# Second product of the feed-forwards: three of four groups by jobs of seven products, and more adding transfers

## The chip, the cores and the metric

The kernel runs on one core of a Trainium2 chip. The core has TensorE (PE, matrix products), VectorE (DVE), ScalarE (ACT), GpSimd (POOL), SyncE (SP, which here only issues transfers) and 16 DMA engines. The metric is the device time of one execution in microseconds, given as the median of several runs.

## The reference

Two decoder layers work on 512 prompt tokens and 32 sample tokens together (T = 544 columns). Layer 0 mixes with a short convolution, layer 1 with retention over four heads. Each layer then adds a feed-forward, which is what the change is about:

```python
def swiglu(x, w_gate, w_up, w_down):
    return (jax.nn.silu(x @ w_gate) * (x @ w_up)) @ w_down
...
        x = x + m
        x = x + swiglu(rmsnorm(x, norm_ffn[i]), ffn_w_gate[i], ffn_w_up[i], ffn_w_down[i])
```

The model width is 1024 (8 tiles of 128), the inner width of the feed-forward 2816 (22 tiles of 128). "First product" below is the pair with w_gate and w_up, "second product" the one with w_down.

## The kernel before, in words

Everything lies transposed: x is eight tiles of 128 features by 544 tokens (line 122). Each fp32 operand of a product is split into a high part, rounded to the fp32r type, and the low remainder. A product then has three terms, high by high, high by low, and low by high, each a matmul of 128 x 128 weights with 272 columns, half of the tokens.

A split can be made in two ways. `split` (195) copies the high part on ScalarE and subtracts it on VectorE. `split_adding` (200) writes the negated high part into the low one on ScalarE and adds the source to it by a transfer from DRAM that accumulates, issued on GpSimd. `mixed` (429) does the first half of a weight's columns in the first way and the second half in the second way.

The first product of a feed-forward (`gate_up`, 603, and class `Job`, 473) does not multiply 2 x 2 blocks by eight products but by seven, in the manner of Strassen and Winograd: the blocks are the two halves of the output tiles and of the input width on the weights' side, and the two halves of the input width and of the tokens on the other. `weights7` (437) loads two matrices of 1024 columns, forms the sums of their blocks on VectorE, and splits everything. `Job.product` (488) issues 4 x 3 = 12 matmuls. A job starts with product 1 (`begin`, 503), goes on with 6, 5, 2 and 7 (`middle`, 508), and closes with 4 and 3 (`end`, 524). `run` (530) chains the jobs: the weights of the next are prepared, the middle of this one is issued, product 1 of the next, and then the end of this one. The results pass from PSUM through `take`: "u1" to "u3" are snapshots of a running sum, "c11" to "c22" finished blocks.

Every inner tile m (0 to 10) stands for the pair of tiles m and m + 11. Two jobs, gate and up, make the hidden activations of one m, and `tail` (586) splits them into `xh` and `xl`, which are free in the feed-forward (`hidden`, 578). The second product is done in groups of three m's: `down` (654), called from `after` (695) once the first job pair of the next group is through, takes for each of the 8 output tiles a weight of 768 columns (`group_weights`, 644), multiplies all six hidden tiles by it in both token halves (`project`, 173), and adds the result to x (`residual`, 280). The last group has two m's (9 and 10) and also prepares what follows the feed-forward.

The pools around this: `wts` has three buffers each for a loaded weight (tag w), its high part (wh) and its low part (wl); one job uses two of each. The pool `sw` has a single buffer for the sums (w2, w4) and their parts. The engines run their instructions in order, but that order is not the order of the text: the framework's planner places instructions by their dependences and its own costs, and `tc.issue_after` forces an order where one is wanted. All plain weight loads go through SP's queue, all adding transfers through GpSimd's.

## Time and profile before

| | us |
|---|---|
| runs of the kernel, median of 3 | 1460.26 |
| lowest, highest | 1457.29, 1460.7 |
| the profiled execution's own time | 1456.52 |
| its span, first to last instruction | 1454.8 |

A profile line of instructions names the source line, the engine, the operation, the tile that is written and the tiles that are read, the shape, and the count; then busy time, the mean of one in ns, and after a second bar the time for which the engine stood idle ahead of them, with what ended most of it. PE is TensorE's matmuls, PEld its weight loads, which overlap them. Matmuls are pipelined: one is listed with some 290 ns, though the next starts 125 ns after it. In the chain of waits a row is start, duration and what ran. In the timeline a row is start, duration, engine, line, operation; a bracket at its end is the idle time ahead of it and its cause. In a table by stretches the columns are named in its first line; a count stands behind each busy time. In a list of transfers stands the size of one and, where known, the median time from issue to landing. In the list of queues stand packets, megabytes, and the share of the 16 DMA engines' span.

### The profile page before, as it was taken

The numbers are of one execution on the slowest core, as the hardware profiler recorded it, in microseconds if no ns is written. First come the engines' busy times: TensorE is split into PE (matmuls) and PEld (weight loads), VectorE is DVE, ScalarE is ACT, GpSimd is POOL, SyncE is SP. The second block draws the span as 40 slices with busy tenths as digits, with TensorE's granted clock in tenths as the row PEclk, the third lists the DMA queues.
The fourth block names the chain that finished last, engine by engine and source line by source line (L and its number), as shares of the span: only waits on it lengthen the run. The fifth ranks groups of instructions, "written<-read, shape, count | busy, mean of one in ns | idle before, by whom it ended". The sixth has DMA issues, their size and how long they took to land.

```text
span 1454.8 us, 26342 instructions
## 1 busy us (share of the span) xinstructions
PE 1440.8 (99%) x10826; PEld 1366.3 (94%) x10826; DVE 985.2 (68%) x1556; ACT 674.5 (46%) x994; POOL 151.5 (10%) x191
## 2 busy tenths in 40 slices
PE   9999999999999999999999999999999999999997
PEld 9999999999999999999877888878899999999997
DVE  5655679847748648677566585666789848759554
ACT  5222466626526436766422313123476626536434
POOL 0100011101101003210000000000111101001002
PEclk9999999999999999999999999999999999999998
DMA  6222246635536434786544373545666635536422
GB/s 226 75 90 90 87 115 145 148 114 125 144 105 143 123 81 126 200 211 192 192 160 159 129 258 122 196 169 186 176 133 156 153 99 134 135 103 153 123 73 77
DMA packets 86041, 204.61 MB, mean 141 GB/s; under 512 B 8832, under 2 KB 26128, under 8 KB 85664
## 3 DMA queue, kind: packets, MB, share of 16 engines
q1 hardware_dynamic: 67744, 165.37, 34.8%
q0 software_dynamic: 15872, 30.75, 12.7%
q10 hardware_dynamic: 2304, 6.79, 1.3%
q8 instruction: 85, 1.39, 0.4%
q14 instruction: 36, 0.29, 0.1%
HBM read 176.14 MB, written 26.75 MB: 139 GB/s over the span
## 4 chain that ended last, share of the span: by engine, by line
PE 93%; issue 2%; DVE 2%; DMA 1%; POOL 1%; ACT 1%; DVEq 0%; POOLq 0%; ACTq 0%
PE sm L494 35%; PE mm L181 34%; PE sm L181 8%; PE sm L1047 2%; PE sm L1048 2%; PE sm L1049 2%; PE sm L169 2%; PE sm L170 1%; PE sm L171 1%; PE sm L1273 1%; PE mm L494 1%; PE mm L1055 1%; PE mm L1291 1%; DMA wl<-in_rtout_dram 0%; PE mm L1222 0%
## 5 line engine op out<-in xcount | busy, mean ns | idle before, releaser
L196 ACT ACTIVATE wh<-w 128x1024 fp32r<-128x1024 f32 (+4 forms) x120 | 109.3, 916 | 293.8 <-PE mm L181 206.0
L494 PE MATMUL sm<-oh,wh 128*128 128x272 f32 x768 | 222.5, 290 | 0.1
L494 PE MATMUL sm<-ol,wh 128*128 128x272 f32 x768 | 221.3, 288 | 0.0
L494 PE MATMUL sm<-oh,wl 128*128 128x272 f32 x768 | 220.8, 287 | 0.0
L282 DVE TENSOR_TENSOR x<-x,mm 128x544 f32<-128x544 f32 x91 | 65.4, 719 | 147.2 <-PE mm L181 147.2
L494 PE MATMUL sm<-oh,h 128*128 128x272 f32 x560 | 161.3, 288 | 0.0
L494 PE MATMUL sm<-oh,l 128*128 128x272 f32 x560 | 160.9, 288 | 0.0
L494 PE MATMUL sm<-ol,h 128*128 128x272 f32 x560 | 160.9, 287 | 0.0
L181 PE MATMUL mm<-xh,wh 128*128 128x272 f32 x756 | 157.5, 290 | 0.0
L181 PE MATMUL mm<-xl,wh 128*128 128x272 f32 x756 | 156.7, 288 | 0.0
L181 PE MATMUL mm<-xh,wl 128*128 128x272 f32 x756 | 156.4, 288 | 0.0
L432 ACT ACTIVATE wh<-w 128x1024 fp32r<-128x1024 f32 x103 | 109.2, 1060 | 89.6 <-PE sm L494 61.7
L494 PEld LDWEIGHTS sm<-oh,wh 128*128 128x128 f32 x768 | 144.2, 188 | 2.4 <-ACT gate L554 1.1
L494 PEld LDWEIGHTS sm<-oh,wl 128*128 128x128 f32 x768 | 144.9, 189 | 0.0
L494 PEld LDWEIGHTS sm<-ol,wh 128*128 128x128 f32 x768 | 144.3, 188 | 0.2 <-DVE ol L197 0.2
L197 DVE TENSOR_TENSOR wl<-w,wh 128x1024 fp32r<-128x1024 f32 (+4 forms) x120 | 127.0, 1063 | 23.2 <-ACT wh L196 21.7
L435 POOL DMA_DIRECT2D wl<-in_ffgu_dram x87 | 75.8, 871 | 635.5 <-ACT wl L434 249.9
L181 PEld LDWEIGHTS mm<-xh,wh 128*128 128x128 f32 x756 | 119.3, 189 | 3.7 <-DVE sl L197 0.9
L181 PEld LDWEIGHTS mm<-xh,wl 128*128 128x128 f32 x756 | 118.7, 189 | 0.3
L181 PEld LDWEIGHTS mm<-xl,wh 128*128 128x128 f32 x756 | 118.9, 189 | 0.0
L197 DVE TENSOR_TENSOR l<-w,h 128x1024 fp32r<-128x1024 f32 x104 | 98.8, 954 | 26.9 <-ACT h L196 25.0
L494 PEld LDWEIGHTS sm<-oh,h 128*128 128x128 f32 x560 | 105.4, 188 | 0.2 <-ACT oh L196 0.2
(319 smaller groups left out, 3318.2 us busy)
## 6 DMA issues: line engine op xcount, KB each, us to landing
w<-in_ffgu_dram SPq DMA_DIRECT2D x88, 512.0 KB
wl<-in_ffgu_dram POOLq DMA_DIRECT2D x87, 256.0 KB, 4.8
w<-in_ffdn_dram SPq DMA_DIRECT2D x96, 192.0 KB
S<-in_rets_dram SPq DMA_DIRECT2D x16, 1024.0 KB
out_rets_dram<-S SPq DMA_DIRECT2D x16, 1024.0 KB
w<-in_cvin_dram SPq DMA_DIRECT2D x21, 512.0 KB
w<-in_rtqk_dram SPq DMA_DIRECT2D x16, 512.0 KB
w<-in_rtg_dram SPq DMA_DIRECT2D x16, 512.0 KB
```

The lines of the kernel that those rows point to most:

```text
L169: nc.tensor.matmul(out, lh, rh, start=start, stop=False, skip_group_check=True)
L170: nc.tensor.matmul(out, lh, rl, start=False, stop=False, skip_group_check=True)
L181: last_product[0] = nc.tensor.matmul(half(pt, hf)[:, :HT], w[:, c], act[k][:, hf * HT : (hf + 1) * HT], start=(first and k == ks[0] and i ...
L196: h = nc.scalar.activation(dh, src, AF.Copy)
L197: last_low[0] = nc.vector.tensor_sub(dl, src, dh.bitcast(F32))
L282: last_residual[0] = nc.vector.tensor_add(xk, xk, p)
L432: nc.scalar.activation(wh, w, AF.Copy)
L435: nc.gpsimd.dma_start(wl[:, n:], src[:, n:], accum_op=ALU.add)
L494: last = nc.tensor.matmul(out, w[:, c], b, start=(first and k == 0 and i == 0), stop=(k == KP - 1 and i == 2), skip_group_check=True,)
L1047: nc.tensor.matmul(out, xh[kt][:, ts_], wh[:, cw], start=(kt == 0), stop=False)
L1048: nc.tensor.matmul(out, xh[kt][:, ts_], wl[:, cw], start=False, stop=False)
L1049: last = nc.tensor.matmul(out, xl[kt][:, ts_], wh[:, cw], start=False, stop=(kt == KT - 1))
```

## The change

The diff does five things.

1. Three of the four groups of the second product are made by jobs of seven products. `group_jobs` builds four jobs a group. A job covers two output tiles of x, the two halves of the inner width, and the two halves of the tokens, so its blocks are 384 columns of weights and its products 3 x 3 = 9 matmuls. The jobs are put into the chain of `run` behind the gate and up jobs of the next group's first m. The finished blocks are added to x in place; the snapshots go into `sqlast` and a new tile `snap`.
2. `tail` forms, for these groups, the four sums of the hidden blocks that the seven products need, and splits all seven operands into the tiles `parts` (the former `xh` and `xl` in one tile) and, for the third m of a group, two tiles of the pool `fp`. The low part of the four sums is made by an adding transfer from SBUF. The tail of m = 3, 6 and 9 is deferred until the group's jobs are through, since they still read the tiles that it writes.
3. `adds`: the gate and up jobs of all m but the first, and all group jobs, make both halves of their first weight's low part with `split_adding` in place of `mixed`.
4. In layer 1's first job, the copies of `weights7`'s sums are placed behind the last negation of the work ahead.
5. In the second mixer, the load of the next head's rotated keys is issued ahead of the load of the gate.

`down` is left for the last group alone and loses its special cases; the spare buffer of the gates computed ahead moves into the tile `snap`. The diff, shortened:

```diff
...
-    xh = [resid.tile([P, T], F32R, tag=f"xh{k}", name=f"xh{k}") for k in range(KT)]
-    xl = [resid.tile([P, T], F32R, tag=f"xl{k}", name=f"xl{k}") for k in range(KT)]
+    parts = resid.tile([P, 2 * KT, T], F32R, tag="parts", name="parts")
+    xh, xl = [[parts[:, i * KT + k, :] for k in range(KT)] for i in range(2)]
+    blocks_of_parts = parts.rearrange("p a (b c) -> p (a b) c", b=2)
...
-    last_low = [None]
+    last_low, last_minus = [None], [None]
...
     def split_adding(dh, dl, w, src):
...
-        nc.scalar.activation(dl, dh.bitcast(F32), AF.Copy, scale=-1.0)
-        nc.gpsimd.dma_start(dl, src, accum_op=ALU.add)
+        last_minus[0] = nc.scalar.activation(dl, dh.bitcast(F32), AF.Copy, scale=-1.0)
+        nc.gpsimd.dma_start(like(dl, src), src, accum_op=ALU.add)
+    def like(t, src):
+        return t.rearrange("p (s c) -> p s c", s=2) if len(src.shape) == 3 else t
...
     def mixed(wh, wl, w, src):
-        n = KP * P
+        n = w.shape[1] // 2
...
-        nc.gpsimd.dma_start(wl[:, n:], src[:, n:], accum_op=ALU.add)
-    def weights7(src1, src2, sw, adding=False, spare=None):
-        n = KP * P
+        nc.gpsimd.dma_start(wl[:, n:], src[:, 1, :] if len(src.shape) == 3 else src[:, n:], accum_op=ALU.add)
+    def weights7(src1, src2, sw, n, adding=False, spare=None, adds=False):
...
-        w4 = (spare or sw).tile([P, n], F32, tag="w4", name=nm("w4"))
+        pool, tag = spare or (sw, "w4")
+        w4 = pool.tile([P, n], F32, tag=tag, name=nm("w4"))
...
-            second_load[0], last_load[0] = last_load[0], nc.sync.dma_start(two[i], (src1, src2)[i])
+            src = (src1, src2)[i]
+            second_load[0], last_load[0] = last_load[0], nc.sync.dma_start(like(two[i], src), src)
...
-        p1 = parts2(2 * n)
-        (split_adding if adding else mixed)(*p1, w1, src1)
-        p2 = parts2(2 * n, sw, ("h2", "l2"))
-        split(*p2, w2)
+        behind, p1, p2 = last_minus[0], parts2(2 * n), parts2(2 * n, sw, ("h2", "l2"))
+        (split_adding if adding or adds else mixed)(*p1, w1, src1)
+        with tc.issue_after(behind.ins) if adding else ExitStack():
+            split(*p2, w2)
...
-        split(*p4, w4)
+        with tc.issue_after(behind.ins) if adding else ExitStack():
+            split(*p4, w4)
...
-        def __init__(self, srcs, operand, sw, take, third=None, spare=None):
+        def __init__(self, srcs, operand, sw, take, third=None, spare=None, ks=range(KP), adds=False):
...
-            self.third, self.spare = third or bank, spare
+            self.third, self.spare, self.ks, self.adds = third or bank, spare, list(ks), adds
...
         def prepare(self, adding=False):
-            self.w = weights7(*self.srcs, self.sw, adding, self.spare)
+            self.w = weights7(*self.srcs, self.sw, len(self.ks) * P, adding, self.spare, self.adds)
         def product(self, out, which, first):
...
-            for k in range(KP):
-                c = slice(k * P, (k + 1) * P)
+            for j, k in enumerate(self.ks):
+                c = slice(j * P, (j + 1) * P)
...
-                        start=(first and k == 0 and i == 0), stop=(k == KP - 1 and i == 2),
+                        start=(first and j == 0 and i == 0), stop=(j == len(self.ks) - 1 and i == 2),
...
+            up_ = c1.enter_context(tc.tile_pool(name=f"ffs{layer}", bufs=1, reuse_waits="tile"))
...
+            turned = {}
+            def seven(m):
+                if m % GROUP < 2:
+                    at = blocks_of_parts[:, 14 * (m % GROUP) : 14 * (m % GROUP) + 14, :]
+                    return [(t[:, 0:1, :], t[:, 1:3, :], t[:, 3:7, :]) for t in (at[:, :7, :], at[:, 7:, :])]
+                rest = [fp.tile([P, 5, HT], F32R, tag="f", name=nm("f")) for _ in range(2)]
+                return [
+                    (t[:, 4:5, :], blocks_of_parts[:, 28 + 2 * i : 30 + 2 * i, :], t[:, 0:4, :]) for i, t in enumerate(rest)
+                ]
             def tail(m, g, u):
-                hs, ls = hidden(m)
-                for i in range(2):
-                    split(hs[i], ls[i], u[:, i, :])
+                if m >= last[0]:
+                    hs, ls = hidden(m)
+                    for i in range(2):
+                        split(hs[i], ls[i], u[:, i, :])
+                    return
+                b, t = [v.rearrange("p a (b c) -> p (a b) c", b=2) for v in (u, g)]
+                (h1, h2, ht), (l1, l2, lt) = seven(m)
+                nc.vector.tensor_sub(t[:, 0:2, :], b[:, 1::2, :], b[:, 0:2, :])
+                split(h1, l1, b[:, 0:1, :])
+                split(h2, l2, b[:, 2:4, :])
+                nc.vector.tensor_sub(t[:, 2, :], b[:, 3, :], t[:, 0, :])
+                nc.vector.tensor_sub(t[:, 3, :], b[:, 2, :], t[:, 2, :])
+                nc.scalar.activation(ht, t, AF.Copy)
+                nc.scalar.activation(lt, ht.bitcast(F32), AF.Copy, scale=-1.0)
+                nc.gpsimd.dma_start(lt, t, accum_op=ALU.add)
+                turned[m] = [
+                    {1: p[0][:, 0, :], 2: p[1][:, 0, :], 3: p[1][:, 1, :],
+                     5: p[2][:, 0, :], 7: p[2][:, 1, :], 6: p[2][:, 2, :], 4: p[2][:, 3, :]}
+                    for p in ((h1, h2, ht), (l1, l2, lt))
+                ]
+            later = {}
+            def group_jobs(ms):
+                c = slice(ms[0] * P, (ms[-1] + 1) * P)
+                src = a["ffdn"][layer].rearrange("(s n) p c -> n p s c", s=2)
+                def job(n):
+                    made = {}
+                    def take(what, p):
+                        if what == "u3":
+                            made[3] = up_.tile([P, HT], F32, tag="snap", name=nm("snap"), bufs=1)
+                            nc.scalar.activation(made[3], p, AF.Copy)
+                            return
+                        if what[0] == "u":
+                            nc.scalar.activation(halves(sqlast)[:, int(what[1]) - 1, :], p, AF.Copy)
+                            return
+                        kt, hf = n + int(what[1]) - 1, int(what[2]) - 1
+                        at = x[kt][:, hf * HT : (hf + 1) * HT]
+                        nc.vector.tensor_add(at, at, p)
+                        if what == "c22":
+                            nc.vector.tensor_add(at, at, made[3])
+                            nc.vector.tensor_add(x[n], x[n], sqlast)
+                    return Job(
+                        [src[n + i][:, :, c] for i in range(2)], lambda k, which: [t[which] for t in turned[k]], sw, take,
+                        lambda: psum()[:, 0, :], ks=ms, adds=True,
+                    )
+                return [job(n) for n in range(0, KT, 2)]
...
-                        tail(m, g, u)
+                        if m and m % GROUP == 0:
+                            later[m] = lambda: tail(m, g, u)
+                        else:
+                            tail(m, g, u)
...
-                        summed(lambda tag="gu"[q]: tile2(tag), (gate, up)[q]),
+                        summed(lambda tag="gu"[q]: tile2(tag), (gate, up)[q]), adds=m > 0,
...
-            def group_weights(n, ms, spare=False):
+            def group_weights(n, ms):
...
-                wh, wl = parts2(2 * len(ms) * P, *((fp, ("f", "f")) if spare else ()))
+                wh, wl = parts2(2 * len(ms) * P)
...
             def down(ms, order):
...
-                g, lead = len(ms), LEAD if ms[-1] == HJ - 1 else 0
+                g = len(ms)
...
-                for n in order[:lead]:
+                for n in order[:LEAD]:
...
-                        wh, wl = group_weights(n, ms, ms[-1] < HJ - 1 and n % 2 == 1)
+                        wh, wl = group_weights(n, ms)
...
-                    if ms[-1] == HJ - 1:
-                        if next_gain is not None and n % KP not in held:
-                            split_x(n, next_gain(n))
-                        square_sum(n, tp, "gu", 4, first=order[0], last=made_in[-1])
-                if next_gain is not None and ms[-1] == HJ - 1:
+                    if next_gain is not None and n % KP not in held:
+                        split_x(n, next_gain(n))
+                    square_sum(n, tp, "gu", 4, first=order[0], last=made_in[-1])
+                if next_gain is not None:
...
-            jobs = [job for m in range(HJ) for job in gate_up(m)]
+            groups = [list(range(m, min(m + GROUP, HJ))) for m in range(0, HJ, GROUP)]
+            last = groups[-1]
+            jobs, behind = [], {}
+            for m in range(HJ):
+                jobs += gate_up(m)
+                if m and m % GROUP == 0:
+                    jobs += group_jobs(groups[m // GROUP - 1])
+                    behind[len(jobs) - 1] = m
...
-            groups = [list(range(m, min(m + GROUP, HJ))) for m in range(0, HJ, GROUP)]
             def after(i):
-                m = i // 2
-                if i % 2 and m % GROUP == 0 and m:
-                    down(groups[m // GROUP - 1], list(range(KT)))
+                if i in behind:
+                    later[behind[i]]()
...
-            last = groups[-1]
...
-                then(tp, fp, sw, operand_tiles, c1.enter_context(tc.tile_pool(name="ffw", bufs=1, reuse_waits="tile")))
+                then(tp, fp, sw, operand_tiles, up_)
...
         def spare():
...
-            return (sw, wp)[turn[0] % 2]
+            return ((sw, "w4"), (wp, "snap"))[turn[0] % 2]
...
-                nc.sync.dma_start(st["gate"][0], gate_made[h])
...
+                nc.sync.dma_start(st["gate"][0], gate_made[h])
...
```

## Prediction

> **What bounds the kernel now.** I read the page's shares first, then the chain of waits in order of time, then the busy times by stretch.
>
> ```profile
> span 1454.8 us, 26342 instructions
> PE 1440.8 (99%) x10826; PEld 1366.3 (94%) x10826; DVE 985.2 (68%) x1556; ACT 674.5 (46%) x994; POOL 151.5 (10%) x191
> ```
>
> TensorE is busy for 99% of the span, so the matmul count sets the time, and any other engine matters only where it makes TensorE wait. The chain shows the feed-forwards' two kinds of stage as unbroken runs of matmuls: L181 x288 is one group of the second product (8 output tiles, 6 inner tiles, 3 terms, 2 halves), and L494 x504 is six jobs of the first product.
>
> ```profile
> 291.16 36.26 PE mm L181 x288
> 327.42 63.19 PE sm L494 x504
> 390.61 35.94 PE mm L181 x288
> 489.75 36.21 PE mm L181 x288
> ...
> 1160.72 36.26 PE mm L181 x288
> 1260.17 35.94 PE mm L181 x288
> 1359.31 36.21 PE mm L181 x288
> ```
>
> 63.19/504 is 0.1254 us a matmul, and the groups run at the same pace (36.14/288 = 0.1255). Nothing waits there now. The stretches below are three gate-and-up pairs, one group of the second product, and two stretches of the gates computed ahead of the second mixer.
>
> ```profile
> core 0: us, PE busy (x) PEld busy (x) DVE busy (x) ACT busy (x) POOL busy (x), PEclk, DMA share, GB/s
> 327.00:390.00 63.00, 63.00 (x505) 63.00 (x504) 51.26 (x80) 41.36 (x64) 9.62 (x11) 1.00 0.58 134
> 390.00:426.00 36.00, 36.00 (x290) 35.99 (x290) 17.21 (x24) 8.48 (x11) 0.88 (x1) 1.00 0.35 116
> 590.00:650.00 60.00, 60.00 (x472) 58.86 (x470) 42.09 (x69) 41.39 (x66) 10.43 (x12) 1.00 0.75 193
> 650.00:690.00 40.00, 39.87 (x289) 37.90 (x290) 30.89 (x61) 24.25 (x37) 3.87 (x6) 1.00 0.72 196
> ```
>
> The clock is 1.00 throughout. In the feed-forward TensorE's weight loads never pause (63.00 of 63, 35.99 of 36). In the two stretches with a DMA share above 0.7 they do: 1.14 us of 60 (1.9%) and 2.1 us of 40 (5.3%). That is the nearest thing in this trace to what the changed stages will be like.
>
> **Matmuls removed.** A group becomes four jobs of seven products, each of 3 inner tiles by 3 terms: 4 x 7 x 9 = 252 matmuls for 288, of the same 272 columns. Over six groups 216 go (10826 to 10610). The six rows sum to 216.8 us; 6 x 252 x 0.1254 is 189.6. **Term: -27.2 us**, if TensorE stays fed.
>
> **What the vector engines must do for it.**
>
> ```profile
> L197 DVE TENSOR_TENSOR f<-w,f 128x768 fp32r<-128x768 f32 x24 | 22.8, 952 | 0.9 <-ACT f L196 0.9
> L196 ACT ACTIVATE f<-w 128x768 fp32r<-128x768 f32 x24 | 20.3, 845 | 66.8 <-PE mm L181 65.8 <-DMA w<-in_ffdn_dram 0.9
> L197 DVE TENSOR_TENSOR sl<-sf,sh 128x384 fp32r<-128x384 f32 x8 | 4.5, 557 | 4.1 <-ACT sh L196 4.1
> L196 ACT ACTIVATE sh<-sf 128x384 fp32r<-128x384 f32 x8 | 4.2, 525 | 11.3 <-DVE sf L1186 11.3
> L557 DVE TENSOR_TENSOR g<-g,sm 128x272 f32<-128x272 f32 x66 | 28.4, 431 | 4.7 <-PE sm L494 3.2 <-ACT g L554 1.4
> L554 ACT ACTIVATE g<-sm 128x272 f32<-128x272 f32 x66 | 26.1, 395 | 53.0 <-PE sm L494 52.9
> L628 DVE TENSOR_TENSOR u<-u,g 128x544 f32<-128x544 f32 x22 | 15.8, 718 | 0.1
> L433 DVE TENSOR_TENSOR wl<-w,wh 128x512 fp32r<-128x512 f32 x103 | 70.8, 688 | 42.7 <-ACT wh L432 41.8
> ```
> ```profile
> 848.73 0.73 DVE L1011 TENSOR_TENSOR rt<-rot,sqlast 128x544 f32<-128x544 f32 x1 [1.20 <-DMA rot<-km]
> 849.37 0.72 DVE L1013 TENSOR_TENSOR rt<-rot,sqlast 128x544 f32<-128x544 f32 x1
> ```
>
> One group job costs VectorE four sums of 384 columns and two 384 splits (6 x 0.557), one 768 split (0.952), five adds of 272 (5 x 0.431) and one of 544 (0.718): 7.2 us by durations, against 63 x 0.1254 = 7.9 us of TensorE. Neighbours overlap by some 0.09 us (848.73 + 0.73 is after 849.37), so with 14 instructions it is nearer 6.0 us, 76%. ScalarE has four passes of 768 (3.38), two of 384 (1.05), three snapshots (1.19): 5.6 us, 71%. Both fit. Before, a group used 17.21 us of VectorE in 36; that slack is spent.
>
> In the gate-and-up pairs the adding transfer takes the first matrix's remaining VectorE half, 2 x 0.688 saved a pair; the new tail costs VectorE two instructions of 544 and three of 272, 2.73 us for the 1.44 of before. Net -0.1 us a pair: VectorE stays at 81% (51.26 of 63), covered. ScalarE gets two wider negations and the tail's two passes of 1088 (about 1.1 each, from 1051 ns for 1024 below) with smaller copies: some 2.8 us more a pair on 41.36/3 = 13.8, so 79% of 21. **Term: 0**; without cover, the group jobs' 4 x 7.2 us still fit in 31.6, so the lower and upper end are both 0 unless something else makes them late.
>
> **The adding transfer of the first parts** is the new wait. Product 1 of a job now needs a whole low part that comes by ScalarE copy, ScalarE negation, an issue on GpSimd, and a transfer. Before the change only product 2, five products later, needs one.
>
> ```profile
> 346.88 1.06 ACT L432 ACTIVATE wh<-w 128x1024 fp32r<-128x1024 f32 x1 [0.99 <-PE sm L494]
> 348.39 0.61 ACT L434 ACTIVATE wl<-wh 128x512 fp32r<-128x512 f32 x1
> 349.30 0.88 POOL L435 DMA_DIRECT2D wl<-in_ffgu_dram  x1 [4.03 <-DVE u L557]
> 354.33 0.29 PE L494 MATMUL sm<-oh,wh 128*128 128x272 f32 x1
> ```
> ```profile
> L203 ACT ACTIVATE wl<-wh 128x1024 fp32r<-128x1024 f32 x7 | 7.4, 1051 | 0.1
> ```
> ```profile
> wl<-in_ffgu_dram POOLq DMA_DIRECT2D x87, 256.0 KB, 4.8
> wl<-in_rtout_dram POOLq DMA_DIRECT2D x4, 512.0 KB, 7.0
> wl<-in_rtqk_dram POOLq DMA_DIRECT2D x2, 512.0 KB, 5.7
> wl<-in_rtqk_dram POOLq DMA_DIRECT2D x4, 256.0 KB, 5.7
> ```
>
> The copy at 346.88 starts when the buffer is released by the previous job's product 4 (TensorE ends the wait of 0.99); product 1 of the next job starts five products later, at 354.33, and reads the low part with its third matmul, 354.58. With the wider negation: 346.88 + 1.06 + 1.05 + 0.30 (348.39 + 0.61 to the issue at 349.30) = 349.3, and 512 KB land after 5.7 to 7.0 us: 355.0 to 356.3, **0.4 to 1.7 us late** in each of 40 gate and up jobs. A group job has 45 matmuls, 5.64 us, plus 0.25, for 0.845 + 0.845 + 0.3 and a transfer of 384 KB (4.8 to 7.0, middle of 256 KB's 4.8 and 512 KB's 5.7: 5.3): 7.3 us, **1.4 late** (0.9 to 3.1) in each of 24. If products run in the text's order, that is 40 x 0.4 + 24 x 1.4 = 50 us, up to 142. But TensorE's order isn't the text's:
>
> ```profile
> 631.24 0.29 PE L494 MATMUL sm<-ol,h 128*128 128x272 f32 x1
> 631.39 0.40 PE L494 MATMUL sm<-oh,wh 128*128 128x272 f32 x1
> ...
> 633.00 0.29 PE L494 MATMUL mm<-xh,h 128*128 128x272 f32 x1
> ...
> 634.50 0.29 PE L494 MATMUL sm<-oh,l 128*128 128x272 f32 x1
> ```
>
> Product 6 of one job has run 5 of 12 matmuls, products 4 and 3 of the job before come between (24 matmuls; the text has them ahead of 6), and then its other 7. The planner fills a wait that it expects. Here 4 and 3 are ready when product 1 would wait: 24 x 0.125 = 3.0 us of cover in a gate job, 2.3 in a group job, more than 1.7 and 1.4, and starting 4 earlier also releases the next buffer earlier. So the wait falls away where the planner's landing is near the real one.
>
> **The DMA engines** are the cover that may go.
>
> ```profile
> q1 hardware_dynamic: 67744, 165.37, 34.8%
> q0 software_dynamic: 15872, 30.75, 12.7%
> ```
>
> Adding transfers take 12.7% x 1454.8 / 30.75 = 6.0 us of all 16 engines a MB. Three pairs get 1.57 MB more (6 x 256 KB) and three tails of 128 x 1088 x 4 bytes (1.67 MB): 36.5 us (0.58 x 63) becomes 56, a share of 0.89. A group gets 4 x 0.59 MB, 14.2 us on 12.6: 0.85 of 31.6. Landings lengthen with the share (256 KB: 4.8 us where it is 0.58, 5.7 where it is 0.75). I price what is left of all waits by the two stretches above: 40 x 10.53 + 24 x 7.9 = 611 us of these jobs lose between 0 (as the gate stages now) and 5.3% (32 us); I take the 60 us stretch, also seven-product jobs, 1.9%. **Term: +11.6 us** (0 to 32).
>
> The Trainium skill, page "DMA: Bandwidth & Descriptors", section "Latency and other measured facts", puts HBM access at 0.2 us on average and 2 us at high load and calls it the main part of a transfer's fixed cost. The trace agrees in direction (4.8 to 5.7 us). By that rule landings would come up to 1.8 us later, an estimate, and the waits in the text's order would be 40 x 2.2 + 24 x 3.2 = 165 us in place of 50, and *slower* below would be 1598.
>
> **Smaller edits.** The snapshots of a group job go into single tiles: the next job's first one waits for the last adds (0.395 + 0.431 + 0.718 and two hand-overs, about 2.2 us behind product 7); product 6, which needs it, comes 27 matmuls, 3.4 us, behind. Behind that snapshot on ScalarE stand the next job's splits. Taken as 0; if VectorE is 2 us late, +0.8 x 24 = 19 us, which the range holds. GpSimd issues 66 more transfers of 0.88 us: 58 us on 151.5 of 1454.8, no bound. In the second mixer the load of the keys (rot) goes onto SP's queue ahead of the gate's:
>
> ```profile
> 852.55 0.68 DVE L1228 TENSOR_TENSOR gate<-gate,mm 128x512 f32<-128x512 f32 x1
> ```
>
> VectorE's wait of 1.20 us at 848.73 can go, in each of two heads (at most 2.4 together), or the gate's load be late at 852.55 instead: -2.4 to +2.4, taken as -0.5. The order of the layer-1 splits and the tile's new grouping move no work: 0.
>
> **Sum.** The profiled execution took 1456.5 us. 1456.5 - 27.2 + 11.6 - 0.5 = 1440.4; the median of the runs, 1460.3, is 3.7 above it, so **1444**.
>
> **The rivals.** *Full gain* (0.22): the planner hides every wait; 1460.3 - 27.2 = 1433. For: weight loads never pause in today's gate stages. Against: the DMA share of 0.85 to 0.89.
> *Forecast* (0.46): 1444, own range 1437 to 1454.
> *DMA-bound* (0.14): all late at the rate of the 40 us stretch, 5.3%; 1460.3 - 27.2 + 32 = 1465. For: the share. Against: that stretch also changes stage.
> *Slower* (0.18): the planner counts the adding transfer as faster than it is, leaves product 1 in the text's place, and TensorE waits there in every job: 1460.3 - 27.2 + 50 = 1483. It decides from 27.2/64 = 0.43 us a job. For: five products are shorter than the chain by these rows. Against: the interleaving.
>
> **How the numbers follow.** About 0.3% (4.4 us) can be told from no change: 1455.9 to 1464.7. Faster: 0.22 + 0.42 of the forecast's 0.46 + 0.02 of DMA-bound = 0.66. Within: 0.02 + 0.06 = 0.08. Slower: 0.18 + 0.08 = 0.26. Low end 1431, the full gain with most of the mixer's 2.4; high end 1472, which leaves out most of *slower*, some 0.15.
>
> **What would show it.** 10610 matmuls; VectorE near 80% in the group stretches; DMA shares of 0.8 to 0.9; product 1 of a job begun and then interrupted by products 4 and 3. A wait of TensorE's weight loads on the low part (wl) of over 0.4 us a job makes the forecast wrong upwards; none makes it 1433.

## The result and the profile after

| | before | after |
|---|---|---|
| median of 4 runs each, us | 1459.66 | 1528.07 |
| lowest, highest | 1457.29, 1460.70 | 1527.27, 1532.42 |
| span of the profiled execution | 1454.8 | 1525.8 |
| mean granted clock of TensorE | 0.997 | 0.988 |

The ratio is 1.0475 with a 95% interval of 1.0459 to 1.0491: slower by 68 us, outside the range. The page of the changed kernel begins like this; the last row is the queue of the adding transfers (packets, megabytes, share of 16 engines).

```profile
span 1525.8 us, 26498 instructions
PE 1444.7 (95%) x10610; PEld 1353.6 (89%) x10610; DVE 1059.1 (69%) x1786; ACT 807.8 (53%) x1198; POOL 215.7 (14%) x257
...
q0 software_dynamic: 28448, 65.42, 25.1%
```

The 216 matmuls are gone, yet TensorE, busy for 99% of the span before, is busy for 95%, and its weight loads for 89% in place of 94%. No other engine has become the bound: VectorE went from 68% to 69%. So TensorE stands still for something, and the view of waits of its weight loads says for what (us in total, times, longest):

```profile
PEld sm L504 <- DMA wl<-in_ffgu_dram: 52.7, 35, 6.0
PEld sm L504 <- DMA wl<-in_ffdn_dram: 27.2, 23, 3.3
```

In the kernel before, neither row exists. L504 is the matmul of `Job.product`, wl here the low part of a job's first weight. Of the 64 jobs whose first weight is made by adding transfers (40 gate and up, 24 of the groups), 58 wait for it, 79.9 us in all. One ordinary gate-and-up job shows how, in the timeline:

```profile
376.12 1.06 ACT L204 ACTIVATE wh<-w 128x1024 fp32r<-128x1024 f32 x1 [1.72 <-PE sm L504]
...
377.36 1.05 ACT L205 ACTIVATE wl<-wh 128x1024 fp32r<-128x1024 f32 x1
...
378.71 0.86 POOL L206 DMA_DIRECT2D wl<-in_ffgu_dram  x1 [3.71 <-ACT wl L205]
...
384.00 0.39 PE L504 MATMUL sm<-oh,wl 128*128 128x272 f32 x1 [0.92 <-DMA wl<-in_ffgu_dram]
```

This is product 1 where the text has it. The chain from the freed buffer takes 384.00 - 376.12 = 7.88 us: copy, negation, issue, and 5.29 us of transfer. TensorE has run out of other work at 383.08, after 6.96 us. Nothing fills the 0.92 us.

The transfers themselves are hardly later than before (list of transfers: size, median us from issue to landing), and the engines are less full than forecast. The stretches are the first product's jobs and a group's four jobs:

```profile
wl<-in_ffgu_dram POOLq DMA_DIRECT2D x41, 512.0 KB, 5.2
wl<-in_ffgu_dram POOLq DMA_DIRECT2D x47, 256.0 KB, 5.2
wl<-in_ffdn_dram POOLq DMA_DIRECT2D x24, 384.0 KB, 5.0
parts<-g POOLq DMA_DIRECT2D x12, 544.0 KB, 6.6
```
```profile
core 0: us, PE busy (x) PEld busy (x) DVE busy (x) ACT busy (x) POOL busy (x), PEclk, DMA share, GB/s
354.00:400.00 46.00, 43.30 (x336) 42.51 (x335) 36.07 (x60) 32.26 (x47) 8.60 (x10) 0.99 0.74 167
405.00:440.00 35.00, 31.75 (x247) 30.89 (x246) 28.20 (x55) 21.40 (x36) 7.25 (x7) 1.00 0.72 167
```

Not every wait is that short. Four take about 5 us each; these are TensorE's rows in the timeline, with one more that is explained below:

```profile
349.10 0.60 PE L504 MATMUL sm<-oh,wl 128*128 128x272 f32 x1 [5.17 <-DMA wl<-in_ffgu_dram]
461.75 0.60 PE L504 MATMUL sm<-oh,wl 128*128 128x272 f32 x1 [4.79 <-DMA wl<-in_ffgu_dram]
567.66 0.39 PE L504 MATMUL sm<-oh,wl 128*128 128x272 f32 x1 [1.31 <-DMA wl<-in_ffgu_dram]
1254.35 0.60 PE L504 MATMUL sm<-oh,wl 128*128 128x272 f32 x1 [5.79 <-DMA wl<-in_ffgu_dram]
1368.89 0.59 PE L504 MATMUL sm<-oh,wl 128*128 128x272 f32 x1 [4.89 <-DMA wl<-in_ffgu_dram]
```

All four stand in the second job behind a group. What ScalarE made and GpSimd issued ahead of the first, that transfer in the chain of waits, and the stretches from the wait on:

```profile
334.89 1.06 ACT L204 ACTIVATE wh<-w 128x1024 fp32r<-128x1024 f32 x1
...
338.15 1.04 ACT L205 ACTIVATE wl<-wh 128x1024 fp32r<-128x1024 f32 x1
...
338.54 0.86 POOL L624 DMA_DIRECT2D parts<-g  x1 [8.05 <-ACT parts L623]
339.49 0.86 POOL L206 DMA_DIRECT2D wl<-in_ffgu_dram  x1
```
```profile
339.49 9.57 DMA wl<-in_ffgu_dram
```
```profile
343.70:349.10 5.40, 0.23 (x2) 0.01 (x1) 0.82 (x2) 0.00 (x0) 0.00 (x0) 0.94 1.04 253
349.10:353.10 4.00, 4.00 (x17) 4.00 (x18) 0.00 (x0) 0.81 (x2) 0.00 (x0) 0.50 0.17 31
353.10:357.10 4.00, 4.00 (x25) 4.00 (x25) 1.43 (x2) 2.53 (x5) 0.86 (x1) 0.72 0.08 12
```

The deferred tail (m = 3) issues its 544 KB just ahead of the next first weight's 512 KB; that one lands 9.57 us after its issue in place of some 5.2, while the DMA share is 1.04 and TensorE idle. From copy to landing this chain takes 349.10 - 334.89 = 14.2 us, 6.3 more than the 7.88 above. The transfer is 4.3 of them (9.57 for 5.29); the other 2.0 lie on ScalarE, where three other passes, the tail's negation among them, stand between the copy and the negation. Then TensorE works at half the granted clock for 4 us and at 0.72 for 4 more, which is 2.0 + 1.1 = 3.1 us lost. The row at 567.66 is the same place behind layer 0's third group. The deferred tail there is that of m = 9, which belongs to the last group, is split on the engines, and makes no transfer: 1.31 us.

**The account.** Spans: 1525.8 - 1454.8 = +71.0 us. The matmuls give -27.2, the waits +79.9, and the lower clock some (0.997 - 0.988) x 1525.8 = +13.7, an estimate, since the mean clock also counts half-clock time in which TensorE stands still. The sum is +66.4; 4.6 us are left unassigned.

### The profile page after: what moved, and what is told of

The parts are those of the page before. It is cut to its first block, busy times and chain, and to the rows that moved or that the text cites. A ratio compares the mean times of both kernels' runs of the same rounds, so it can differ in the third digit from the quotient of the medians.

```text
span 1525.8 us, 26498 instructions
## 1 busy us (share of the span) xinstructions
PE 1444.7 (95%) x10610; PEld 1353.6 (89%) x10610; DVE 1059.1 (69%) x1786; ACT 807.8 (53%) x1198; POOL 215.7 (14%) x257
## 3 DMA queue, kind: packets, MB, share of 16 engines
q0 software_dynamic: 28448, 65.42, 25.1%
## 4 chain that ended last, share of the span: by engine, by line
PE 51%; issue 23%; DMA 14%; DVE 6%; POOL 4%; ACT 1%; POOLq 0%; DVEq 0%; ACTq 0%
PE mm L183 15%; PE sm L504 13%; DMA wl<-in_ffgu_dram 10%; PE sm L183 6%; DMA wl<-in_ffdn_dram 2%; PE sm L1127 2%; PE sm L1126 2%; PE sm L1128 2%; POOL wl L206 2%; POOL wl L441 2%; PE mm L504 2%; PE sm L171 2%; PE sm L173 1%; PE sm L172 1%; PE sm L1352 1%
## 5 line engine op out<-in xcount | busy, mean ns | idle before, releaser
L504 PE MATMUL sm<-oh,wl 128*128 128x272 f32 x768 | 228.4, 297 | 45.1 <-DMA wl<-in_ffgu_dram 44.8
L504 PE MATMUL sm<-oh,wh 128*128 128x272 f32 x768 | 225.3, 294 | 0.1
L504 PE MATMUL sm<-ol,wh 128*128 128x272 f32 x768 | 224.0, 292 | 0.4 <-DVE ol L199 0.4
L198 ACT ACTIVATE wh<-w 128x1024 fp32r<-128x1024 f32 (+3 forms) x96 | 89.0, 933 | 218.8 <-PE mm L183 130.9
L504 PEld LDWEIGHTS sm<-oh,wl 128*128 128x128 f32 x768 | 148.1, 193 | 52.9 <-DMA wl<-in_ffgu_dram 52.7
L504 PE MATMUL sm<-oh,h 128*128 128x272 f32 x560 | 163.1, 291 | 0.6 <-ACT g L564 0.3
L504 PE MATMUL sm<-ol,h 128*128 128x272 f32 x560 | 162.0, 290 | 0.0
L504 PE MATMUL sm<-oh,l 128*128 128x272 f32 x560 | 161.3, 289 | 0.0
L183 PE MATMUL mm<-parts,wh 128*128 128x272 f32 x936 | 157.7, 290 | 0.0
L199 DVE TENSOR_TENSOR l<-w,h 128x1024 fp32r<-128x1024 f32 (+3 forms) x152 | 135.0, 890 | 29.9 <-ACT h L198 28.9
L504 PEld LDWEIGHTS sm<-oh,wh 128*128 128x128 f32 x768 | 146.9, 191 | 3.5 <-ACT g L564 1.3
L504 PEld LDWEIGHTS sm<-ol,wh 128*128 128x128 f32 x768 | 147.5, 192 | 0.7 <-DVE ol L199 0.7
L183 PEld LDWEIGHTS mm<-parts,wh 128*128 128x128 f32 x936 | 133.5, 189 | 3.8 <-DVE sl L199 0.9
L198 ACT ACTIVATE h<-w 128x1024 fp32r<-128x1024 f32 (+3 forms) x152 | 119.3, 786 | 30.7 <-PE mm L504 15.1
L199 DVE TENSOR_TENSOR wl<-w,wh 128x1024 fp32r<-128x1024 f32 (+3 forms) x96 | 104.2, 1091 | 27.8 <-ACT wh L198 25.9
L204 ACT ACTIVATE wh<-w 128x1024 fp32r<-128x1024 f32 (+1 forms) x71 | 70.0, 987 | 78.9 <-PE sm L504 61.4
L504 PE MATMUL sm<-parts,wh 128*128 128x272 f32 x560 | 110.6, 290 | 0.0
L504 PEld LDWEIGHTS sm<-oh,h 128*128 128x128 f32 x560 | 107.4, 192 | 1.4 <-ACT oh L198 0.6
L504 PEld LDWEIGHTS sm<-oh,l 128*128 128x128 f32 x560 | 107.1, 191 | 0.0
L504 PEld LDWEIGHTS sm<-ol,h 128*128 128x128 f32 x560 | 106.9, 191 | 0.0
L504 PE MATMUL sm<-parts,wl 128*128 128x272 f32 x280 | 84.1, 300 | 22.4 <-DMA wl<-in_ffdn_dram 22.2
L438 ACT ACTIVATE wh<-w 128x1024 fp32r<-128x1024 f32 (+1 forms) x87 | 86.8, 998 | 31.2 <-PE sm L504 24.1
```

The costliest lines, as they stand in the source:

```text
L183: last_product[0] = nc.tensor.matmul(half(pt, hf)[:, :HT], w[:, c], act[k][:, hf * HT : (hf + 1) * HT], start=(first and k == ks[0] and i ...
L198: h = nc.scalar.activation(dh, src, AF.Copy)
L199: last_low[0] = nc.vector.tensor_sub(dl, src, dh.bitcast(F32))
L204: nc.scalar.activation(dh, w, AF.Copy)
L438: nc.scalar.activation(wh, w, AF.Copy)
L504: last = nc.tensor.matmul(out, w[:, c], b, start=(first and j == 0 and i == 0), stop=(j == len(self.ks) - 1 and i == 2), skip_group_check= ...
```

## The experiments

Five theories stand in the expectations. **W**: product 1 waits for its whole low part, since the planner leaves it in the text's place. **D**: the DMA engines are too full, and the transfers late for that reason. **V**: VectorE is overloaded by the group jobs. **Q**: the deferred tail's transfer, ahead of a first weight's on GpSimd's queue, makes the long waits. **L**: the long waits are due to the group jobs' shorter products. Each result stands against runs of the kernel before that were made beside it. Their medians were 1461.22 us for experiments 1 (first result), 2 and 3 (first result), 1458.87 for 4 (first and third result), 5 and 6, and 1458.64 for the rest. A result without a range is a single execution; those of the kernel before lie up to 0.4% apart.

**1. No whole adds.** The first weights of all jobs are made by `mixed` again, half of the low part on VectorE; the seven-product groups stay.

```diff
-                        lambda: psum()[:, 0, :], ks=ms, adds=True,
+                        lambda: psum()[:, 0, :], ks=ms, adds=False,
...
-                        summed(lambda tag="gu"[q]: tile2(tag), (gate, up)[q]), adds=m > 0,
+                        summed(lambda tag="gu"[q]: tile2(tag), (gate, up)[q]), adds=False,
```

> The changed kernel with `mixed` for every first weight, in gate and up jobs and in group jobs, as before the change; the seven-product groups and the tails' adding transfers stay. Theory W (product 1 waits for a whole low part that comes by copy, negation, issue and transfer, and stands in the text's place): the weight loads' waits for wl (52.7 us first product, 27.2 us second) go to under 5 us and the clock's loss with them: 1433 to 1440 us. Theory D (the DMA engines are too full for the transfers to land in time): the adding bytes fall only from 65.4 to about 50 MB against 30.8 before the change, so a third of the waits stay: 1470 to 1490. Theory V (the group jobs and tails overload VectorE): 64 more half splits of 0.56 to 0.69 us make it worse: waits for VectorE take the place, above 1480.

Measured: 1431.43 us (1430.04 to 1433.63), ratio 0.9798 (0.9779 to 0.9818). That is just below W's 1433 to 1440 and far from the values of D and V, 97 us below the changed kernel and faster than the kernel before. Its page, and its stretches (one layer's jobs, a group, three gate-and-up pairs):

```profile
span 1429.8 us, 26580 instructions
PE 1416.9 (99%) x10610; PEld 1337.9 (94%) x10610; DVE 1087.0 (76%) x1850; ACT 787.1 (55%) x1198; POOL 207.4 (15%) x257
...
q0 software_dynamic: 25376, 50.22, 20.9%
```
```profile
205.00:530.00 325.00, 324.28 (x2579) 322.69 (x2579) 285.21 (x501) 229.67 (x363) 67.30 (x76) 1.00 0.71 160
295.00:326.00 31.00, 31.00 (x251) 31.00 (x249) 29.22 (x59) 22.77 (x40) 6.61 (x8) 1.00 0.71 170
326.00:390.00 64.00, 63.81 (x508) 63.40 (x507) 55.79 (x95) 45.56 (x71) 13.54 (x16) 1.00 0.75 166
```

The DMA share is 0.71 to 0.75, as in the changed kernel (0.72 to 0.74), and TensorE never waits for a low part of these jobs: the same fullness without the waits speaks against D. VectorE carries more than in the changed kernel, 29.22 us of 31 in the group (94%), and TensorE's weight loads still run through: V is out. Repeated, beside experiment 7:

> e1 again beside e12, on the same chip and with the same runs of the kernel before: 1430 to 1433 us.

1431.92 us (1431.02 to 1432.49), ratio 0.9818 (0.9804 to 0.9831).

**2. Whole adds in the groups alone, and in gate and up alone.** One of the two lines of the edit above at a time.

> First weights of gate and up jobs by `mixed`, those of group jobs by the whole adding transfer. W: 23 waits of 1.2 us on the second product's low part come back and nothing else: 1433 + 27 = 1460, to 1468. D: between e1 and the changed kernel by bytes (9 of 20 MB): about 1490. V: as e1.

> First weights of gate and up jobs (all but m = 0) by the whole adding transfer, those of group jobs by `mixed`. W: the 53 us of waits in 35 first-product jobs, and the clock's loss behind the longest of them (about 15 us): 1490 to 1505. D: about 1505 too, so this run tells W from D only with e2.

Measured: 1460.16 and 1494.84 us. Against 1431.4 without any, the groups' adds cost 28.7 and the gates' 63.4; together 92.1 of the 96.6 us that both cost. The waits of weight loads, of the first and then of the second kernel:

```profile
PEld sm L504 <- DMA wl<-in_ffdn_dram: 23.8, 19, 3.4
```
```profile
PEld sm L504 <- DMA wl<-in_ffgu_dram: 54.7, 37, 6.1
```

Each part brings its own waits, of the size that it has in the changed kernel (27.2 and 52.7), and the first kernel is where W put it, not where D did. The second lies where W put it, but D's value is too near to tell the two apart.

**3. The end of a job ahead of the next one's start, in the text.** If TensorE keeps this order, products 4 and 3 (24 matmuls, 18 in a group job) run ahead of product 1 as more cover.

```diff
             job.middle()
-            if nxt is not None:
+            if nxt is not None and not nxt.adds:
                 nxt.begin()
             job.end()
+            if nxt is not None and nxt.adds:
+                nxt.begin()
```

> All transfers as in the changed kernel; only the text's order of products: 4 and 3 of a job ahead of product 1 of the next where that one adds. W: 24 matmuls (3.0 us) or 18 (2.3 us) of cover against waits of 1.5 and 1.2 us: the waits shrink to the few long ones behind a group (4 of 4.8 us) and to product 6's wait for the first snapshot, some 0.5 us a job: 1450 to 1475. D: the same bytes in the same stages, no change: 1515 to 1530.

Measured: 1499.7 us, above W's range. The planner doesn't keep the text's order: in many jobs it moved product 1 ahead of 4 and 3 again. The waits on the low part fell from 79.9 to 33.9 us in 23 places (31.2 of them on gate and up weights); others came in, for the snapshots on ScalarE, of which the largest is shown:

```profile
PEld sm L504 <- DMA wl<-in_ffgu_dram: 31.2, 20, 4.6
...
PEld sm L504 <- ACT g L566: 6.2, 25, 0.8
```

So the order was forced:

```diff
+                self.last = last
...
+            if nxt is not None and nxt.adds:
+                with tc.issue_after(job.last.ins):
+                    nxt.begin()
```

> e4 again, but the order is forced: product 1 of the next job is issued behind the last matmul of products 4 and 3, where e4 left it to the planner, which put it ahead again in many jobs. W: from the release of the buffer (product 4) to product 1's third matmul now lie at least six products, 9 us in a gate job and 6.8 in a group job, plus the wait of product 6 for the first snapshot: gate waits go, group waits fall under 0.5 us, some 0.5 us a job for the snapshot comes in, the four long ones stay with the clock's loss: 1475 to 1495. D or any theory by which these transfers cannot land in time: 1500 and above, waits for wl as in e4.

Measured: 1512.0 us. As a time this is outside W's range and where D has it; but D's sign, waits on the low part as in the run before, isn't there:

```profile
PEld sm L504 <- ACT g L568: 37.1, 42, 2.0
PEld sm L504 <- ACT u L568: 15.8, 42, 0.9
...
PEld sm L504 <- DMA wl<-in_ffgu_dram: 7.3, 8, 1.2
```

```profile
370.29 0.39 PE L504 MATMUL sm<-oh,wh 128*128 128x272 f32 x1 [1.76 <-ACT g L568]
```

Two things follow. With the same adding transfers (65.42 MB) and two products more of cover, the low part is late in 8 places and for 7.3 us in place of 79.9: the transfers are not too slow, product 1 is too early. And product 1 between 7 and 4 had a purpose. The last row, from the timeline, is product 4 directly behind product 7: it adds to the same PSUM bank and must wait until ScalarE has taken the snapshot of it. Such waits for g and u come to 52.9 us. Moving product 1 back trades one wait for another.

**4. The tail's low part by VectorE.** The deferred tail (and the others) makes no transfer; the whole adds stay.

```diff
-                nc.scalar.activation(lt, ht.bitcast(F32), AF.Copy, scale=-1.0)
-                nc.gpsimd.dma_start(lt, t, accum_op=ALU.add)
+                nc.vector.tensor_sub(lt, t, ht.bitcast(F32))
```

> The changed kernel, its adding transfers of first weights and all, but the low part of the tail's four sums by VectorE in place of negation and adding transfer. Theory Q (the four waits of 4.8 to 5.8 us behind a group come from the deferred tail's 544 KB transfer, issued on GpSimd just ahead of the next job's, and TensorE runs at half clock for some 4 us or more behind each): the long waits shrink to about 1.5 us, the clock's loss goes: 1528 - 4 x 3.5 - 12, 1495 to 1508. Rival L (the job behind a group waits long because a group job's five products are shorter): unchanged, 1520 to 1530. Where DMA volume mattered (theory D), 10 MB fewer would shorten all waits alike.

Measured: 1489.44 us, 38.6 below the changed kernel, somewhat below Q's range and far from L's. The waits:

```profile
PEld sm L504 <- DMA wl<-in_ffgu_dram: 34.3, 35, 2.0
PEld sm L504 <- DMA wl<-in_ffdn_dram: 24.2, 20, 1.8
```

The longest fell from 6.0 to 2.0 us, the count is nearly as it was (55), and the mean clock is 0.999. The waits account for 79.9 - 58.5 = 21.4 of the 38.6 us, the clock for some 0.011 x 1488 = 16. L is out as the cause of the long waits: the group jobs kept their short products here, and the long waits went. The edit takes the tail's negation off ScalarE as well, so it prices negation and transfer together. With the tail merely one job later in the text the result is less clear:

```diff
-                if i in behind:
-                    later[behind[i]]()
+                if i - 1 in behind:
+                    later[behind[i - 1]]()
```

> The changed kernel with the deferred tails of m = 3, 6 and 9 put off by one more job, so that their transfer no longer stands beside the transfers and loads of the job right behind a group. Q (the burst behind a group: the tail's 544 KB, the next first weight's 512 KB and its loads at once, share 0.93 in 338.5 to 349 us): the four long waits fall to about 1.5 us and the half clock behind them goes: 1490 to 1505. If the long waits come from the first job behind a group itself: 1520 to 1530.

1516.91 us, between the two expectations. The longest waits fell only to 4.2 us:

```profile
PEld sm L504 <- DMA wl<-in_ffgu_dram: 48.7, 36, 4.2
```

In the order that GpSimd follows, the tail's transfer moved little: in all four places it now stands just behind the same first weight's transfer, where it stood just ahead. The first place:

```profile
334.67 0.86 POOL L206 DMA_DIRECT2D wl<-in_ffgu_dram  x1 [6.25 <-ACT g L564]
336.50 0.86 POOL L624 DMA_DIRECT2D parts<-g  x1 [0.97 <-ACT parts L623]
```

The chain from copy to landing takes 10.0 us there (331.88 to 341.87) in place of 14.2: 2.4 less in the landing, and 1.8 less on ScalarE, where the tail's passes no longer stand between copy and negation. TensorE's idle time there fell from 5.17 to 2.94 us; in the other three it lay between 4.8 and 5.8 and now lies between 3.0 and 4.0. So the tail's transfer ahead on the queue makes a part of the long waits, and its passes on ScalarE another; this run supports Q in part only. And without whole adds, where the tail's transfer has nobody to hold up, taking it away (the edits of experiments 1 and 4 together) gives nothing:

> e1 with the tail's low part by VectorE too: no adding transfer but those of the halves that the kernel before had. W: TensorE waited for nothing in e1, so nothing to win: 1430 to 1433. Theory V: VectorE, at 0.87 of the feed-forward in e1, gets 1.1 us more a pair and becomes late: 1440 to 1455. If GpSimd's queue still cost e1 something: below 1429.

1431.44 us (1430.1 to 1434.67), ratio 0.9808 (0.9791 to 0.9824), the same as experiment 1, with still more work on VectorE.

**5. One adding transfer, but of the first half.** `mixed` with its halves exchanged: product 1 needs a transfer as in the changed kernel, but one of half the size, with a shorter negation ahead, while VectorE makes the second half.

```diff
...
+        nc.vector.tensor_sub(wl[:, n:], w[:, n:], wh[:, n:].bitcast(F32))
+        nc.scalar.activation(wl[:, :n], wh[:, :n].bitcast(F32), AF.Copy, scale=-1.0)
+        nc.gpsimd.dma_start(wl[:, :n], src[:, 0, :] if len(src.shape) == 3 else src[:, :n], accum_op=ALU.add)
...
-        (split_adding if adding or adds else mixed)(*p1, w1, src1)
+        (split_adding if adding else mixed_turned if adds else mixed)(*p1, w1, src1)
```

> The changed kernel with only half of each first weight's low part by an adding transfer, as before the change, but the first half, which product 1 needs; VectorE makes the second half. Bytes as in e1. Theory W with a landing that goes with the size (4.8 us for 256 KB): the chain is 1.06 + 0.63 + 0.30 + 4.8 = 6.8 us for 7.7 in a gate job, no wait, and about 0.5 us late in a group job: 1445 to 1460. W with a landing of 5.2 us whatever the size: only the half negation is saved, 0.42 us a gate job and 0.32 a group job of the 80 us: 1490 to 1505. Theory D: as e1, 1431, since the bytes are those of e1.

Measured: 1461.73 us. The waits and the landings:

```profile
PEld sm L512 <- DMA wl<-in_ffgu_dram: 24.3, 6, 5.8
```
```profile
wl<-in_ffgu_dram POOLq DMA_DIRECT2D x87, 256.0 KB, 5.1
wl<-in_ffdn_dram POOLq DMA_DIRECT2D x48, 192.0 KB, 4.3
```

Only 6 waits are left. Four of them, each about 5 us, are the long ones in the second job behind a group; the waits make up 24.3 of the 30 us by which this kernel stands above experiment 1, and a granted clock of 0.50 behind the long ones (336.93 to 340.04 us behind the first) fits the rest. The short waits are gone. A negation of 512 columns in place of 1024 (0.61 and 1.05 us) and a landing 0.1 us sooner in a gate job, 0.7 in a group job, have a part in it. The other part is TensorE's order: in the gate and up jobs looked at (225 to 285 us) it is the text's again, where in the changed kernel a part of product 6 stands ahead of product 4 in every second one (more on this below). Experiment 4's kernel has the text's order there, too. What each part is worth wasn't separated. The time lies just above what size alone would give, since that estimate left the long waits out, and far below the value without an effect of size; D's value, 1431, is missed as well.

**6. Whole adds in the kernel before.** No seven-product groups; only gate and up of m > 0 get the whole adds.

```diff
-            self.w = weights7(*self.srcs, self.sw, adding, self.spare)
+            self.w = weights7(*self.srcs, self.sw, adding or self.adds, self.spare)
...
-                        summed(lambda tag="gu"[q]: tile2(tag), (gate, up)[q]),
+                        summed(lambda tag="gu"[q]: tile2(tag), (gate, up)[q]), adds=m > 0,
```

> The kernel before with one part of the change alone: whole adding transfers for the first weights of gate and up jobs of m > 0, groups by plain products. W: waits of about 1 us in 40 jobs and none of the long ones, since no tail transfer stands ahead: 1495 to 1510. D: the DMA share stays under 0.75 in the gate stretches, where e1 ran without waits: 1460.

Measured: 1481.19 us, below W's range and far above D's value. So the adds alone make the kernel before slower by 22.3 us, with no tail's transfer, and a DMA share of 0.57 over a stretch of layer 0's feed-forward (first row). The waits are on the low part and, for 6.1 us, on snapshots:

```profile
300.00:500.00 200.00, 195.55 (x1545) 193.52 (x1544) 126.21 (x188) 103.06 (x146) 20.95 (x24) 1.00 0.57 141
```

```profile
PEld sm L494 <- DMA wl<-in_ffgu_dram: 12.7, 22, 1.9
...
PEld sm L494 <- ACT u L554: 6.1, 8, 1.0
```

12.7/22 is 0.6 us a wait, in 22 of 40 jobs, where the changed kernel has 1.0 in ordinary ones. Why the other 18 don't wait wasn't followed up.

**7. The two small orders undone** (layer 1's splits and the load of the rotated keys), in the kernel of experiment 1.

```diff
-        with tc.issue_after(behind.ins) if adding else ExitStack():
+        with ExitStack():
...
+                nc.sync.dma_start(st["gate"][0], gate_made[h])
...
-                nc.sync.dma_start(st["gate"][0], gate_made[h])
```

> e1 without the two small edits: the gate's load ahead of the keys' in the second mixer, and layer 1's first splits left free, as before the change. The term was -0.5, between -2.4 and +2.4: 1430 to 1435 here, the difference to e11 under 2.4 us.

1430.47 us (1429.23 to 1433.05), ratio 0.9811 (0.9797 to 0.9824), which overlaps with the 0.9818 (0.9804 to 0.9831) of experiment 1 repeated beside it: no difference that can be measured.

The kernel of experiment 1 is the version that beats both: 1.8 to 2.0% below the kernel before.

## Why the prediction was wrong

**Matmuls removed, -27.2 us: right.** Experiment 1 has 10610 matmuls and is 26.7 us (the repeat) to 29.8 us below the kernel before.

**VectorE and ScalarE at nothing: right**, although the load was under-sized. I took 6.0 us a group job, 76%, and named 80% as the sign; a group stretch shows 28.20 of 35, 81%. But that stretch contains TensorE's waits. Its 247 matmuls alone take 247 x 0.1254 = 31.0 us, of which 28.20 are 91%, so the 7.2 us worked out from plain durations (7.2 of 7.9, 91%) was the better estimate. (The job has 13 instructions on VectorE, not the 14 that I counted.) The term is 0 all the same.

**The adding transfer of the first parts: the step that failed.** It ran: "The planner fills a wait that it expects. Here 4 and 3 are ready when product 1 would wait", and "So the wait falls away where the planner's landing is near the real one." What landing the planner reckoned with isn't on record, but the order that it made is. In 58 of 64 jobs TensorE stood at product 1's third matmul, and in 54 of them it had taken up product 1 with nothing in between. The interruption by products 4 and 3, which I had named as the sign, is there only in the four jobs with the long waits. Ten matmuls of these products stand in front of the third there (342.26 to 343.64 us in the first), 1.3 us of cover, and about 5 us are still missing. The row that I leaned on showed product 6 interrupted; it showed that the planner can interleave, not that it knows when a transfer lands. The interleaving even took cover away: between 376.05, where product 4's last matmul has been issued, and 383.08 the table by stretches has 57 matmuls, two of them the last of product 4,

```profile
376.05:383.08 7.03, 7.03 (x57) 6.81 (x55) 5.20 (x6) 6.63 (x9) 0.86 (x1) 1.00 0.91 172
```

so 55, where the text's order has 62 (products 3, 6, 5, 2, 7 and two of product 1): seven matmuls of product 6 had been pulled ahead of product 4, 0.88 us. Product 1's second matmul starts at 382.79; without a wait the third would have followed at 382.92, 6.80 us after the copy's start, and not the 7.70 (354.58 - 346.88) that I had read from before.

***Slower*, at 0.18, had the mechanism.** Its price, 50 us, was off in three terms. A gate or up job with a shorter wait stands for about 1.0 us, not 0.4 (in the view of weight loads the four long waits are 21.5 us, and (52.7 - 21.5) / 31 = 1.0). These 31 jobs are of several kinds. In 16, where the products before stand in the text's order, the mean is 0.56 us, near my 0.4. In 7, where product 6 had been pulled ahead of product 4, it is 1.1: the landing was shorter than I took (5.2 us, not 5.7 to 7.0), but the cover had shrunk by 0.9. In the 6 that come first behind a group it is 1.8 to 2.0, since their cover is a group job's 45 matmuls, which I had set against the group job's own weights alone; the last 2, behind a third group, wait 1.5. A group job waits 27.2/23 = 1.18 us, not 1.4. And the four waits of about 5 us with the clock behind them weren't in it at all; experiment 4 prices them, with all else that the tail's negation and transfer cost, at 38.6 us. I had counted the tail's 544 KB in the DMA share, but hadn't asked which transfer stands behind it on GpSimd's queue, nor what waits for that one.

**The DMA engines, +11.6 us: the wrong measure.** I forecast shares of 0.89 and 0.85; they are 0.74 and 0.72, partly since the waits stretch the time: experiment 1, with 15.2 MB less, has 0.71 to 0.75 without any. Adding transfers did grow as worked out (30.75 to 65.42 MB), but the loss doesn't follow the share. *DMA-bound* is false as a rate over 611 us; it holds in the four stretches of some 5 us behind the groups where the share is 1.01 to 1.04. *Full gain* is what the kernel does without the whole adds (1433 forecast, 1431.4 measured).

By the rule of the Trainium skill, page "DMA: Bandwidth & Descriptors", section "Latency and other measured facts", which the prediction weighed, landings would have come up to 1.8 us later. The medians for 256 KB went from 4.8 to 5.2 us, 0.4 later; the trace agrees in direction only.

**The smaller edits** (-0.5, between -2.4 and +2.4) can't be told from nothing (experiment 7). **The snapshots** of a group job at 0 held: the changed kernel has no wait for sqlast or snap. With product 1 forced away from between 7 and 4 (experiment 3) they cost 8.7 us, and those of the gate and up jobs 52.9.

## What to carry to other kernels

When a producer moves from an engine to a transfer, work out for each consumer the chain (free buffer, passes, issue, landing) against the instructions that truly stand ahead of it, and count a planner's reordering as cover only if the trace shows it for that consumer and that kind of producer. Give a transfer to the operand that is needed last: here the second half of a weight can come by one at no cost, while the whole, whose first half the first product needs, cost 22 us even in the kernel without the group jobs. List what is issued just ahead on the same queue, and what stands between the passes of the chain on the engine that makes them: one large transfer ahead made the neighbour's landing nearly twice as long, and three passes in between added 2.0 us.

## What the hardware showed that I hadn't expected

**The clock falls behind a wait.** Behind each of the four long waits the granted clock is 0.50 to 0.55 for 4 us (first: 17 matmuls in 4 us, where 32 are usual). It also fell behind a short one, and not behind another of nearly the same length:

```profile
330.86 0.39 PE L504 MATMUL sm<-oh,wl 128*128 128x272 f32 x1 [1.77 <-DMA wl<-in_ffgu_dram]
```
```profile
330.90:334.90 4.00, 4.00 (x20) 4.00 (x21) 1.14 (x2) 1.52 (x3) 0.00 (x0) 0.57 0.92 258
396.40:400.40 4.00, 4.00 (x33) 4.00 (x34) 1.37 (x3) 1.10 (x4) 1.12 (x2) 1.00 0.95 205
```

The first stretch lies behind that wait of 1.77 us (clock 0.57, 20 matmuls), the second behind one of 1.53 (1.00, 33). What may tell them apart is where they lie. The half clock lasts 3.41 us behind the first and 6.83 behind each long wait, and these stretches begin whole multiples of 3.41 us apart (331.42 and 348.49: five). On the grid of these steps the two waits look like this:

```profile
328.02:331.43 3.41, 1.64 (x13) 1.42 (x12) 3.33 (x6) 1.58 (x3) 0.86 (x1) 1.00 1.05 262
392.88:396.29 3.41, 1.88 (x16) 1.67 (x14) 2.97 (x6) 3.36 (x4) 0.49 (x1) 1.00 0.87 207
```

The wait of 1.77 us lies within one step, in which TensorE is busy for 1.64 us; that of 1.53 begins in the second row's step, busy for 1.88, and ends in the next. So what counts seems to be how much of one step is idle, not how long the wait is; that is a reading of these rows, which no run here tests, and where the limit lies stays open. The Trainium skill, page "TensorE: Matmul & The Clock Gate", section "What's actually happening", has the clock halved after an idle window of about 3.4 us and restored after about 3.4 us of work. The trace agrees for the four long waits (4.8 to 5.8 us), and not for the one of 1.77.

**A landing hardly depends on the size here, but on what runs beside it.** In the changed kernel 512, 384 and 256 KB land after 5.2, 5.0 and 5.2 us (medians); the same 512 KB take 9.57 behind the tail's 544 KB, where the DMA share is 1.04 at 253 GB/s. In experiment 5 the first weight's 256 KB in the same place take 9.2 (327.70 to 336.93), and where the tail's transfer stands just behind (experiment 4) the 512 KB take 7.2. How much of that is the order on the queue and how much the full engines wasn't separated.

**An engine at 94% can be harmless.** VectorE's 29.22 us of 31 in experiment 1 cost TensorE nothing, while DMA engines at 0.72 to 0.74, with one transfer in each job needed too early, left TensorE waiting for 80 us.
